# RMSNorm and QKV projection: 2x2 block products on row-tile pairs replaced by 3x2-by-2x3 block products on row-tile triples

## The chip, the cores and the metric

The kernel runs on one core of one Trainium2 chip. The metric is the device time of one execution in microseconds (us). The kernel before takes 352.87 us (median of three runs, 352.66 to 354.76).

## The reference

`x` has shape 8 x 1024 x 768 (8192 rows), `w_qkv` 768 x 2304, all in f32; `gamma` is one per column of `x`.

```
rms = np.sqrt(np.mean(x ** 2, axis=-1, keepdims=True) + eps)
x_norm = x / rms * gamma
return np.matmul(x_norm, w_qkv).astype(np.float32)
```

## The kernel before, in words

The 8192 rows are 64 row tiles of 128 rows. The contraction of 768 is six chunks (`ko`) of 128, and TensorE takes one 128x128 block of transposed x as its weights and streams a block of w past it.

The weights arrive as 16 pieces of f32 (`load_w`, L442), are multiplied by gamma and rounded to bf16 (`conv`, L448 to L452) into the tile `w_b`.

**Head.** Row tiles 0 to 3 are computed plainly: cast to bf16, transposed on TensorE (`tr`, L480), multiplied chunk by chunk with 512-wide blocks of `w_b` (`mm`, L516), scaled by 1/rms at the eviction (`evac`). Meanwhile the largest weight of each of three column groups of 768 is found (`bound`, `fold`, `bound_tr`, `bound_top`, `bound_all`), the group is divided by a scale made from it and written as four f16 quarters of 384 (k) x 384 (n) (`quad`, L616 to L618), and four differences of quarters are formed (`tsum`, L624).

**Pairs.** The other 60 row tiles go in 30 pairs. Each tile of x is loaded (`load_x`, L437), its sum of squares taken on ScalarE (`pstat`, L634), scaled to f16 on VectorE (`pcast`, L648) and transposed by a DMA (`pxbar`, L652; four of these tiles on TensorE, `ptr`, L671). A pair is a 2x2 arrangement of blocks (two row tiles, two halves of k); four sums of these blocks are formed, most on GpSimd (`osum`, L666). For each pair and each column group, seven block products (`product`, L686) replace the eight of a plain 2x2 product. A product is three matmuls of 384 columns. Products 1, 6, 7 and 4 accumulate one after the other in one PSUM bank; product 2 has a second bank, 5 and 3 a third. Between two products of a bank the running sum is read out: `hold` (L693 on VectorE, L695 on ScalarE) copies it, scaled, to an f32 tile `pp`; `join` (VectorE, L711) adds a scaled bank to a held one and writes a quarter of the result; `last` (ScalarE, L715) writes a quarter without an addition. Per pair and group that is seven readings. `pstore` (L740) stores 768 columns of a row tile; results lie in 12 tiles `ot` or in the spent `w_b`.

**The order.** `PLAN` is a list of operations with a time each; from pair 15 on, a fixed pattern over `SLOT` adds them. All are sorted by that time, and this one order is the order of every engine's queue; the engines run freely against each other and wait on semaphores. All DMAs but gamma's and one last store are issued by the SP queue. The last product is cut in two halves (`end_piece`, L722; `end_out`, L730 to L734), stored from two queues.

Of the kernel before, what the change touches and what calls it, by code (L numbers as in the profile page):

```python
# [9 lines left out]

PIECES = [(0, 2, 0, 512), (2, 3, 0, 512), (3, 4, 0, 512), (4, 5, 0, 512), (5, 6, 0, 512), (0, 2,
          512, 512), (2, 4, 512, 512), (4, 6, 512, 512), (0, 2, 1024, 512), (2, 4, 1024, 512), (4,
          6, 1024, 512), (0, 2, 1536, 512), (2, 4, 1536, 512), (4, 6, 1536, 512), (0, 3, 2048,
          256), (3, 6, 2048, 256)]

HEAD_END = 166.25
STEADY = 15

PLAN = [
    (0.000, "load_x", 1), (1.160, "load_x", 0), (1.580, "load_x", 2), (5.030, "cast", 0, "DVE"), (5.031, "load_w", 4),  # L20
    (5.032, "load_w", 1), (6.820, "cast", 2, "DVE"), (6.821, "cast", 1, "ACT"), (6.822, "stat", 0),
    (6.823, "load_w", 2), (6.824, "load_w", 3), (6.825, "gamma_in"), (6.826, "idle", 14, 512), (6.827, "tr", 1),
    (7.480, "conv", 4, 5, "DVE"), (7.481, "tr", 0), (7.482, "cp", 0, "ACT"), (7.483, "tr", 2),
    (7.484, "cp", 1, "ACT"), (8.050, "mm", 0, 0, "5"), (8.141, "conv", 1, 2, "DVE"), (8.266, "mm", 1, 0, "5"),
    (8.267, "load_x", 3), (8.801, "conv", 2, 3, "DVE"), (8.802, "cp", 2, "ACT"), (8.803, "mm", 0, 0, "2"),
    (8.926, "mm", 1, 0, "2"), (9.142, "mm", 2, 0, "5"), (9.371, "mm", 2, 0, "3"), (9.372, "stat", 1),
    (9.461, "conv", 3, 4, "DVE"), (9.587, "mm", 0, 0, "3"), (9.803, "mm", 1, 0, "3"), (10.031, "mm", 0, 0, "4"),
    (10.032, "recip", 0), (10.451, "stat", 3), (10.452, "load_w", 0), (11.772, "conv", 0, 1, "POOL"),
    (11.773, "mm", 2, 0, "4"), (11.774, "conv", 0, 0, "ACT"), (11.775, "cast", 3, "DVE"), (11.776, "mm", 1, 0, "4"),
    (11.777, "tr", 3), (12.612, "mm", 1, 0, "01"), (13.043, "mm", 0, 0, "01"), (13.044, "load_w", 6),  # L30
    (13.045, "load_w", 7), (13.046, "stat", 2), (13.047, "load_w", 5), (13.092, "conv", 6, 2, "POOL"),
    (13.093, "load_w", 10), (13.094, "cp", 3, "DVE"), (13.095, "bound", 0, 1, "DVE"), (13.831, "conv", 6, 3, "DVE"),
    (13.971, "bound", 0, 0, "ACT"), (14.261, "recip", 2), (14.262, "mm", 2, 0, "012"), (14.263, "mm", 3, 0, "012345"),
    (14.264, "load_w", 8), (14.361, "recip", 1), (15.571, "evac", 2, 0, "ACT"), (15.572, "recip", 3),
    (15.573, "load_w", 9), (17.054, "conv", 10, 5, "POOL"), (17.055, "mm", 0, 512, "23"),
    (17.056, "mm", 2, 512, "23"), (17.057, "conv", 7, 4, "DVE"), (17.058, "conv", 7, 5, "DVE"),
    (17.059, "mm", 1, 512, "45"), (17.060, "mm", 0, 512, "54"), (17.145, "mm", 3, 512, "45"),
    (17.146, "conv", 5, 1, "DVE"), (17.147, "evac", 3, 0, "ACT"), (17.576, "mm", 2, 512, "45"),
    (17.577, "load_w", 15), (17.578, "evac", 1, 0, "ACT"), (17.579, "conv", 5, 0, "DVE"),
    (18.008, "mm", 1, 512, "23"), (18.009, "bound", 1, 0, "ACT"), (18.010, "load_x", 5),  # L40
    (18.011, "bound", 0, 2, "DVE"), (18.554, "fold", 0), (18.555, "mm", 1, 512, "01"), (18.871, "bound_tr", 0),
    (18.872, "conv", 10, 4, "POOL"), (18.873, "evac", 0, 0, "DVE"), (18.971, "conv", 8, 0, "ACT"),
    (19.364, "bound_top", 0), (19.365, "load_x", 4), (19.366, "conv", 8, 1, "POOL"), (19.367, "mm", 3, 512, "01"),
    (19.695, "conv", 9, 3, "POOL"), (19.724, "bound_all", 0), (19.844, "mm", 2, 512, "01"), (20.044, "scales", 0),
    (20.045, "load_w", 14), (20.275, "mm", 1, 1024, "01"), (20.707, "mm", 3, 1024, "45"),
    (20.708, "evac", 1, 512, "ACT"), (21.139, "mm", 2, 1024, "01"), (21.140, "conv", 9, 2, "POOL"),
    (21.141, "evac", 2, 512, "ACT"), (21.142, "load_x", 7), (21.570, "mm", 0, 512, "01"),
    (22.002, "mm", 0, 1024, "23"), (22.003, "bound", 1, 2, "DVE"), (22.434, "mm", 3, 512, "23"),
    (22.435, "load_x", 6), (22.866, "mm", 2, 1024, "45"), (23.297, "mm", 3, 1024, "01"),
    (23.298, "quad", 0, "b22", "ACT"), (23.299, "quad", 0, "b12", "POOL"), (23.300, "bound", 1, 1, "DVE"),  # L50
    (23.301, "pstat", 5), (23.729, "mm", 3, 1024, "23"), (24.035, "fold", 1), (24.036, "pstat", 4),
    (24.037, "conv", 15, 3, "POOL"), (24.215, "conv", 15, 5, "ACT"), (24.216, "evac", 3, 512, "DVE"),
    (24.217, "mm", 0, 1024, "01"), (24.645, "prms", 2), (24.646, "bound_tr", 1), (24.845, "evac", 3, 1024, "DVE"),
    (24.846, "mm", 0, 1024, "45"), (24.895, "conv", 15, 4, "ACT"), (24.896, "load_w", 13), (24.897, "load_w", 12),
    (25.144, "mm", 1, 1024, "23"), (25.145, "quad", 0, "b11", "POOL"), (25.146, "load_w", 11),
    (25.325, "evac", 0, 512, "ACT"), (25.925, "evac", 0, 1024, "ACT"), (25.926, "mm", 0, 2048, "345"),
    (25.927, "mm", 1, 2048, "345"), (25.928, "bound_top", 1), (26.231, "bound_all", 1), (26.351, "mm", 1, 1024, "45"),
    (26.352, "conv", 14, 1, "POOL"), (26.353, "precip", 2), (26.354, "pcast", 5), (26.705, "conv", 14, 2, "DVE"),
    (26.965, "pcast", 4), (26.966, "pstat", 6), (26.967, "mm", 2, 1024, "23"), (26.968, "load_x", 15),
    (27.515, "tsum", 0, "t1", "DVE"), (27.516, "evac", 1, 1024, "ACT"), (27.517, "ptr", 5),  # L60
    (28.095, "conv", 13, 4, "ACT"), (28.215, "pcp", 5, "DVE"), (28.216, "conv", 14, 0, "POOL"),
    (28.217, "mm", 3, 2048, "345"), (28.218, "mm", 0, 2048, "012"), (28.735, "conv", 13, 5, "ACT"),
    (28.855, "osum", 2, "s1", "DVE"), (28.856, "mm", 3, 2048, "012"), (28.857, "mm", 2, 2048, "345"),
    (28.884, "ptr", 4), (29.244, "mm", 1, 2048, "012"), (29.572, "mm", 2, 2048, "012"),
    (29.573, "evac", 3, 2048, "DVE"), (29.574, "load_x", 12), (29.575, "pstat", 7),
    (29.818, "store", 3, 2, 2048, 256), (29.819, "scales", 1), (30.238, "load_x", 8), (30.239, "pcp", 4, "DVE"),
    (30.240, "quad", 0, "b21", "POOL"), (30.345, "evac", 0, 2048, "ACT"), (30.498, "evac", 1, 2048, "DVE"),
    (30.898, "evac", 2, 2048, "DVE"), (30.899, "mm", 1, 1536, "45"), (30.900, "conv", 12, 3, "POOL"),
    (31.038, "store", 1, 2, 2048, 256), (31.039, "conv", 12, 2, "POOL"), (31.040, "conv", 11, 0, "POOL"),
    (31.041, "quad", 1, "b21", "POOL"), (31.042, "mm", 3, 1536, "45"), (31.043, "mm", 3, 1536, "23"),  # L70
    (31.458, "store", 2, 2, 2048, 256), (31.459, "mm", 2, 1536, "23"), (31.460, "bound", 2, 1, "DVE"),
    (31.461, "conv", 11, 1, "ACT"), (31.462, "quad", 1, "b11", "ACT"), (31.626, "mm", 3, 1536, "01"),
    (32.575, "prms", 3), (32.576, "product", 2, 0, 1), (32.978, "evac", 2, 1024, "DVE"), (32.979, "product", 2, 0, 2),
    (33.033, "mm", 2, 1536, "45"), (33.034, "hold", 2, 0, "a", "p1", "ACT"), (33.638, "precip", 3),
    (33.639, "store", 0, 2, 2048, 256), (33.738, "join", 2, 0, 0, 0, "b", "p1"), (34.288, "pcast", 6),
    (34.289, "load_x", 17), (34.290, "load_x", 16), (34.291, "load_x", 11), (34.998, "osum", 2, "s2", "DVE"),
    (34.999, "mm", 0, 1536, "23"), (35.000, "mm", 1, 1536, "01"), (35.001, "mm", 2, 1536, "01"),
    (35.002, "bound", 2, 2, "ACT"), (35.003, "mm", 0, 1536, "01"), (35.191, "mm", 1, 1536, "23"),
    (35.192, "bound", 2, 0, "ACT"), (35.193, "quad", 1, "b22", "POOL"), (35.623, "product", 2, 0, 5),
    (35.624, "tsum", 0, "t2", "DVE"), (36.110, "mm", 0, 1536, "45"), (36.111, "pcast", 7),  # L80
    (36.568, "osum", 2, "s4", "DVE"), (36.569, "product", 2, 1, 1), (36.570, "pxbar", 6),
    (36.888, "osum", 2, "s3", "DVE"), (36.889, "evac", 1, 1536, "ACT"), (37.029, "product", 2, 1, 2),
    (37.030, "load_x", 23), (37.125, "hold", 2, 0, "c", "p5", "ACT"), (37.126, "quad", 1, "b12", "POOL"),
# [285 lines left out]
def kernel(  # L369
# [137 lines left out]
    def width(t, n0):  # L507
        return min(NT, N - n0)

# [328 lines left out]
```

## Time and profile before

| What | Value |
|---|---|
| median of three runs | 352.87 us |
| the profiled execution: span from first to last instruction | 352.0 us, 0.87 below the median; no other time of this execution is given |
| TensorE (PE) busy | 341.8 us, 97% |
| VectorE (DVE) busy | 265.3 us, 75% |
| ScalarE (ACT) busy | 242.1 us, 69% |
| GpSimd (POOL) busy | 118.0 us, 34% |
| granted TensorE clock | 1.000 |
| bytes moved by DMA | 119.19 MB, mean 339 GB/s |

How to read it: busy time of PE counts a matmul up to its modelled end, which overlaps the next one; the rate of the matmuls is read from their starts in the timeline. The DMA share is the busy share of the core's 16 DMA engines, summed over packets, so that it can pass 1.0 where packets overlap. SP has no compute; its rows are DMA issues.

### The profile page before, as it was taken

How to read it: one execution, taken by the hardware profiler on the slowest of the kernel's cores; microseconds unless marked ns; L12 is line 12 of the kernel's file. 1: busy time of each engine (PE TensorE's matmuls, PEld its weight loads, DVE VectorE, ACT ScalarE, POOL GpSimd, SP SyncE). 2: the span in 40 equal slices, each digit the busy share in tenths (PEclk: the TensorE clock that was granted, in tenths of full speed). 3: DMA queues.
4: the chain of work that ended last, by engine and by line, in shares of the span. 5: the costliest groups of instructions: out<-in, count | busy, mean ns of one | idle time of the engine just before them, and what ended most of it. 6: DMA issues, size and time to landing. Idle time of an engine off the chain costs nothing.

```text
span 352.0 us, 6558 instructions
## 1 busy us (share of the span) xinstructions
PE 341.8 (97%) x2079; PEld 201.4 (57%) x2082; DVE 265.3 (75%) x504; ACT 242.1 (69%) x497; POOL 118.0 (34%) x130
## 2 busy tenths in 40 slices
PE   6799999999999999999999999999999999999995
PEld 2346555666666666656666565656666666666663
DVE  2689989888788987786776859677686867767663
ACT  4999988966776756757758575766757677564543
POOL 0187237413123105244404444251614444163000
PEclk9999999999999999999999999999999999999999
DMA  7998999999999999999999999999999999998565
GB/s 267 391 383 295 311 405 309 331 313 374 314 301 374 338 411 340 371 384 314 359 374 316 404 341 365 346 386 354 356 344 326 369 327 373 314 380 301 202 260 223
DMA packets 86238, 119.19 MB, mean 339 GB/s; under 512 B 49206, under 2 KB 51132, under 8 KB 86204
## 3 DMA queue, kind: packets, MB, share of 16 engines
q1 hardware_dynamic: 86048, 118.68, 100.8%
q8 instruction: 16, 0.26, 0.3%
q14 instruction: 18, 0.15, 0.1%
q10 hardware_dynamic: 156, 0.10, 0.1%
HBM read 32.25 MB, written 75.50 MB: 306 GB/s over the span
## 4 chain that ended last, share of the span: by engine, by line
PE 92%; ACT 4%; DVE 1%; issue 1%; DMA 1%; DVEq 0%; ACTq 0%
PE pm L686 85%; PE pm L516 5%; PE pm L555 2%; ACT sq L576 1%; ACT xT L458 1%; DVE ot L711 1%; DMA g<-in_gamma_dram 1%; ACT ot L534 0%; ACT sq L467 0%; ACT pp L695 0%; PE pm L671 0%; DVE xb L648 0%; ACT w_b L450 0%; PE pm L480 0%; DVE pp L693 0%
## 5 line engine op out<-in xcount | busy, mean ns | idle before, releaser
L686 PE MATMUL pm<-wq,su 128*128 128x384 f16 x1080 | 203.8, 326 | 0.3 <-DVE pp L693 0.3
L695 ACT ACTIVATE pp<-pm,sc 128x384 f32<-128x384 f32 x207 | 116.5, 581 | 75.0 <-PE pm L686 72.7
L686 PE MATMUL pm<-wq,xT 128*128 128x384 f16 x807 | 159.3, 326 | 1.0 <-DVE ot L711 0.6
L686 PEld LDWEIGHTS <-su 128*128 128x128 f16 x1080 | 105.5, 98 | 70.1 <-issue 0.5
L711 DVE SCALAR_TENSOR_TENSOR ot<-pm,sc,pp 128x384 f32<-128x384 f32 x172 | 100.3, 611 | 23.6 <-PE pm L686 21.4
L686 PEld LDWEIGHTS <-xT 128*128 128x128 f16 x807 | 78.7, 98 | 54.1 <-issue 1.1
L666 POOL TENSOR_TENSOR su<-xT 128x384 f16<-128x384 f16 x52 | 49.6, 956 | 154.3 <-DMA xT<-xb 82.5
L711 DVE SCALAR_TENSOR_TENSOR w_b<-pm,sc,pp 128x384 f32<-128x384 f32 x98 | 58.1, 613 | 28.5 <-PE pm L686 24.5
L693 DVE TENSOR_SCALAR pp<-pm,sc 128x384 f32<-128x384 f32 x63 | 38.4, 614 | 19.1 <-PE pm L686 18.8
L634 ACT ACTIVATE sq<-x_t 128x768 bf16<-128x768 f32 x60 | 50.1, 835 | 2.1 <-DMA x_t<-in_x_dram 2.0
L648 DVE TENSOR_SCALAR xb<-x_t,rstd 128x768 f16<-128x768 f32 x60 | 41.0, 688 | 0.5
L715 ACT ACTIVATE ot<-pm,sc 128x384 f32<-128x384 f32 x48 | 27.5, 576 | 11.7 <-PE pm L686 11.7
L715 ACT ACTIVATE w_b<-pm,sc 128x384 f32<-128x384 f32 x41 | 23.4, 576 | 9.3 <-PE pm L686 9.3
L666 POOL TENSOR_TENSOR su<-su,xT 128x384 f16<-128x384 f16 x24 | 22.7, 948 | 19.6 <-DVE su L666 9.5
L516 PE MATMUL pm<-w_b,xT 128*128 128x512 bf16 (+1 forms) x117 | 25.1, 358 | 1.9 <-ACT w_b L450 0.9
L666 POOL TENSOR_TENSOR su<-xT,su 128x384 f16<-128x384 f16 x24 | 22.4, 933 | 8.7 <-DVE su L666 7.0
L516 PEld LDWEIGHTS <-xT 128*128 128x128 bf16 x120 | 11.2, 98 | 12.5 <-ACT xT L458 1.7
L452 POOL TENSOR_SCALAR w_b<-wq,g_sb 128x512 bf16<-128x512 f32 (+1 forms) x13 | 8.5, 665 | 18.0 <-DMA wq<-in_w_qkv_dram 18.0
L634 ACT ACTIVATION_READ_ACCUMULATOR sq<-x_t 128x1 f32 x60 | 11.5, 192 | 0.0
L618 POOL TENSOR_SCALAR wq<-w_b,inv 128x1152 f16<-128x1152 bf16 x8 | 10.1, 1266 | 3.2 <-issue 2.6
L638 ACT ACTIVATE rms<-ssq,eps_sb 128x2 f32<-128x2 f32 x30 | 8.8, 293 | 0.0
L573 DVE TENSOR_REDUCE bnd<-w_b 128x1 f32<-128x1536 bf16 x5 | 8.6, 1742 | 0.1
(57 smaller groups left out, 94.9 us busy)
## 6 DMA issues: line engine op xcount, KB each, us to landing
out_dram<-ot SPq DMA_DIRECT2D x110, 384.0 KB, 4.8
out_dram<-w_b SPq DMA_DIRECT2D x68, 384.0 KB, 5.0
x_t<-in_x_dram SPq DMA_DIRECT2D x64, 384.0 KB, 5.5
wq<-in_w_qkv_dram SPq DMA_DIRECT2D x10, 512.0 KB, 9.1
out_dram<-ot SPq DMA_DIRECT2D x8, 512.0 KB, 7.4
wq<-in_w_qkv_dram SPq DMA_DIRECT2D x4, 256.0 KB, 6.0
xT<-xb SPq DMA_TRANSPOSE x56, 5.0
wq<-in_w_qkv_dram SPq DMA_DIRECT2D x2, 384.0 KB, 9.5
```

The source lines that it names most:

```text
L516: nc.tensor.matmul(out=PM[t, n0][:, :nl], lhsT=XT[t][:, ko, :], rhs=w_b[:, ko, n0:n0 + nl], start=(b == 1), stop=(b == KO))
L573: nc.vector.tensor_reduce(out=o, in_=v, axis=mybir.AxisListType.XY, op=amax, apply_absolute_value=True)
L618: nc.gpsimd.tensor_scalar(out=o, in0=quad_view(c, q), scalar1=INV[c], scalar2=1.0, op0=mult, op1=mult)
L634: nc.scalar.activation(out=sq, in_=X[t], func=AF.Square, accum_out=SS[p][:, t % 2:t % 2 + 1])
L638: nc.scalar.activation(out=r, in_=SS[p], func=AF.Sqrt, scale=inv_k, bias=eps_sb)
L648: nc.vector.tensor_scalar(out=XB[t], in0=X[t], scalar1=SS[t // 2][:, t % 2:t % 2 + 1], scalar2=None, op0=mult)
L666: (nc.vector if eng == "DVE" else nc.gpsimd).tensor_tensor(out=block(p, q), in0=block(p, x), in1=block(p, y), op=op)
L686: nc.tensor.matmul(out=PB[k][:, :CW], lhsT=block(p, a)[:, ko, :], rhs=WQ[c, b][:, ko, :], start=(first and ko == 0), stop=(ko == KO // 2 - ...
L693: nc.vector.tensor_scalar(out=o, in0=pb, scalar1=SC[c], scalar2=None, op0=mult)
L695: nc.scalar.activation(out=o, in_=pb, func=AF.Copy, scale=SC[c], bias=0.0)
L711: nc.vector.scalar_tensor_tensor(out=result(p, c, i, j), in0=PB[p, c, bank][:, :CW], scalar=SC[c], in1=PART[p, c, held], op0=mult, op1=add)
L715: nc.scalar.activation(out=result(p, c, 1, 0), in_=PB[p, c, "a"][:, :CW], func=AF.Copy, scale=SC[c], bias=0.0)
```

## The change

The whole PLAN and most helpers are rewritten. The head still computes row tiles 0 to 3 plainly in bf16, now in 384-wide blocks (144 matmuls in place of 93 of 512 and 24 of 256). The other 60 row tiles go in 20 triples. A triple `g` is 384 consecutive rows; row tile `i` of it holds rows 3p+i. A triple is 3x2 blocks of x (three row tiles, two halves of k), a column half `c` (1152 columns) is 2x3 blocks of w, and 15 block products give the nine result blocks for which a plain product takes 18. The weights are scaled once per column half; 13 sums of weight blocks are formed per half (`bsum`), and 11 sums of x blocks per triple (`osum`). The 15 products run in two chains, each accumulating in one PSUM bank; after each product the bank is read once (`hold` on ScalarE six times, `join` on VectorE nine times), directly into the result tile, and a join adds in place. A triple is loaded by one DMA and transposed by one DMA; stores are 1152 columns of a row tile. Each engine's order is the order of the new PLAN, written out for all triples; PSUM banks, sum tiles and result tiles are numbered by hand. No TensorE transposes and no split last product remain after the head.

Counts, from the new PLAN: 600 products (1800 matmuls of 384 columns), 240 holds, 360 joins, 220 osums (207 on POOL, 13 on DVE), 26 bsums (18 DVE, 8 POOL), 60 pcasts (30 DVE, 30 ACT), 60 pstats. SP issues 24 loads of x, 12 of w, 20 transposes and 128 stores.

The core of the diff (the old helpers of the same names, printed above, go):

```diff
-PRODUCTS = {1: ("a11", "b11"), 2: ("a12", "b21"), 3: ("s4", "b22"), 4: ("a22", "t4"), 5: ("s1", "t1"), 6: ("s2", "t2"),
-            7: ("s3", "t3")}
+A_OF = (6, 7, 8, 9, 10, 11, 5, 12, 3, 4, 13, 14, 15, 16, 0)
+B_OF = (6, 7, 1, 5, 8, 9, 10, 11, 12, 13, 14, 15, 16, 17, 18)
+FIRST = (2, 10)
+CHAIN = (0, 0, 0, 1, 1, 1, 0, 0, 0, 1, 1, 1, 0, 1, 1)
+HW = 3 * CW
+    PS = many(8, [P, 512], f32, "ps", banks)
+    XI = many(3, [P, 3, K], f32, "xi")
+    XB = many(2, [P, 3, K], f16, "xb")
+    XT = many(3, [P, 3 * KO, P], f16, "xt")
+    SU = many(26, [P, H, P], f16, "su")
+    OUT = [spent[:, HW * j:HW * (j + 1)] for j in range(KO)] + many(8, [P, HW], f32, "ot")
+    def rows(v, g):
+        r0 = P * (N_HEAD + 3 * g)
+        return v[r0:r0 + 3 * P, :].rearrange("(p i) n -> p i n", i=3)
+    def load_t(eng, g, slot):
+        xi[g] = XI[slot]
+        nc.sync.dma_start(out=xi[g], in_=rows(xf, g))
+    def pxbar(eng, g, i0, i1, *slot):
+        nc.sync.dma_start_transpose(out=place(g, slot)[:, KO * i0:KO * i1, :], in_=xb[g][:, i0:i1].rearrange("p i k -> p (i k)"))
+    def a_block(g, i):
+        return xt[g][:, H * i:H * (i + 1), :] if i < 6 else su[g, i]
+    def osum(eng, g, f, op, i, j, slot):
+        su[g, f] = SU[slot]
+        plus(eng, su[g, f], a_block(g, i), a_block(g, j), add if op == "add" else sub)
+    def bsum(eng, c, f, op, i, j, slot):
+        wf[c, f] = WH[slot]
+        plus(eng, wf[c, f], wf[c, i], wf[c, j], add if op == "add" else sub)
+    def product(eng, g, c, r, *bank):
+        if bank:
+            po[g, c, CHAIN[r]] = PS[bank[0]][:, :CW]
+        a, b, o = a_block(g, A_OF[r]), wf[c, B_OF[r]], po[g, c, CHAIN[r]]
+        for k in range(H):
+            nc.tensor.matmul(out=o, lhsT=a[:, k, :], rhs=b[:, k, :], start=(r in FIRST and k == 0), stop=(k == H - 1),
+                             skip_group_check=True)
+    def hold(eng, g, c, r, i, sign, *slot):
+        to(eng, part(g, c, i, slot), po[g, c, CHAIN[r]], (sc if sign > 0 else nsc)[c])
+    def join(eng, g, c, r, i, sign, j, other, *slot):
+        nc.vector.scalar_tensor_tensor(out=part(g, c, i, slot), in0=po[g, c, CHAIN[r]], scalar=(sc if sign > 0 else nsc)[c],
+                                       in1=part(g, c, j), op0=mult, op1=add if other > 0 else sub)
+    def pstore(eng, g, c, i):
+        nc.sync.dma_start(out=rows(of, g)[:, i, HW * c:HW * (c + 1)], in_=ot[g, c, i])
```

Two places of the new PLAN, each item being operation, engine, triple, column half, product. The first is where the products begin:

```
bsum DVE 0 10 add 3 7 13;product PE 0 0 2 4;osum POOL 0 15 add 0 1 6;product PE 0 0 10 5;osum DVE 0 9 add 7 13 7;
hold ACT 0 0 2 2 -1 10;bsum DVE 0 13 sub 9 17 14;osum POOL 0 14 add 2 3 8;hold ACT 0 0 10 8 1 11;product PE 0 0 12;
```

The second is from the repeated part, with a piece of one triple's joins in a row:

```
pxbar SP 13 0 3 0;product PE 11 0 5;join DVE 11 0 0 1 -1 2 -1;hold ACT 11 1 12 0 1;product PE 11 1 11;
osum POOL 12 9 add 7 13 6;join DVE 11 0 5 5 -1 4 -1;product PE 11 0 1;hold ACT 11 1 11 3 1;product PE 11 1 7;
osum POOL 12 14 add 2 3 14;join DVE 11 0 1 4 1 4 1;product PE 11 0 4;join DVE 11 1 7 6 -1 8 -1;product PE 11 0 8;
osum POOL 12 15 add 0 1 4;join DVE 11 0 4 2 1 2 1;product PE 11 1 13;product PE 11 1 6;osum POOL 12 16 sub 4 14 2;
```

## The prediction

> **What bounds the kernel now.** I read the page's busy line and the chain of waits first, then the groups by line, the timeline for the step of a matmul and for the turn of a PSUM bank, and the windows for the DMA share.
>
> ```profile
> span 352.0 us, 6558 instructions
> ...
> PE 341.8 (97%) x2079; PEld 201.4 (57%) x2082; DVE 265.3 (75%) x504; ACT 242.1 (69%) x497; POOL 118.0 (34%) x130
> ...
> PE 92%; ACT 4%; DVE 1%; issue 1%; DMA 1%; DVEq 0%; ACTq 0%
> ...
> L686 PE MATMUL pm<-wq,su 128*128 128x384 f16 x1080 | 203.8, 326 | 0.3 <-DVE pp L693 0.3
> L695 ACT ACTIVATE pp<-pm,sc 128x384 f32<-128x384 f32 x207 | 116.5, 581 | 75.0 <-PE pm L686 72.7
> L686 PE MATMUL pm<-wq,xT 128*128 128x384 f16 x807 | 159.3, 326 | 1.0 <-DVE ot L711 0.6
> ```
>
> PE carries 92% of the chain, and its product matmuls waited 1.3 us in all, while ACT waited 72.7 us for them. TensorE is the bound; the readers have slack.
>
> ```profile
> 306.01 0.65 PE L686 MATMUL pm<-wq,su 128*128 128x384 f16 x3
> ...
> 309.42 0.65 PE L686 MATMUL pm<-wq,su 128*128 128x384 f16 x3
> ```
>
> Between these two starts lie seven products (21 matmuls): 3.41 us, so 0.1625 us a matmul and 0.4875 a product. The means of 326 ns include the modelled drain.
>
> ```profile
> 340.62 0.65 PE L686 MATMUL pm<-wq,xT 128*128 128x384 f16 x3
> 340.82 0.62 DVE L693 TENSOR_SCALAR pp<-pm,sc 128x384 f32<-128x384 f32 x1 [0.72 <-PE pm L686]
> ...
> 341.80 1.77 DVE L711 SCALAR_TENSOR_TENSOR ot<-pm,sc,pp 128x384 f32<-128x384 f32 x3 [0.36 <-PE pm L686]
> ...
> 346.67 1.14 DVE L711 SCALAR_TENSOR_TENSOR w_b<-pm,sc,pp 128x384 f32<-128x384 f32 x2 [0.23 <-PE pm L686]
> ...
> 347.35 0.66 PE L722 MATMUL pm<-wq,xT 128*128 128x192 f16 x6 [0.22 <-DVE w_b L711]
> ```
>
> The reader starts 0.20 us after the next product may start (340.82 against 340.62), takes about 0.60, and PE goes on 0.07 after it (346.67 + 0.61 to 347.35). So a bank turns in 0.87 us: two other products between two of one bank (0.975) hide it, one (0.4875) leaves 0.38 open, none 0.87. Readings in a row come each 0.58 us (three in 1.77).
>
> ```profile
> 10.00:30.00 20.00, 18.48 (x96) 8.64 (x99) 15.85 (x31) 18.99 (x37) 10.03 (x14) 1.00 1.05 386
> ...
> 80.00:100.00 20.00, 20.00 (x125) 12.05 (x124) 16.85 (x34) 13.88 (x31) 5.35 (x6) 1.00 1.10 345
> ...
> 180.00:300.00 120.00, 119.36 (x735) 71.61 (x733) 88.40 (x163) 81.96 (x177) 45.06 (x48) 1.00 1.07 355
> ...
> 340.00:346.00 6.00, 6.00 (x39) 3.61 (x38) 3.28 (x7) 3.63 (x7) 0.00 (x0) 1.00 0.60 241
> ```
>
> The columns are length, busy PE, weight loads, DVE, ACT, POOL, clock, DMA share and GB/s. The DMA share is 1.07 in the steady part, so DMA is the second resource that is nearly spent.
>
> **Part 1, matmuls.** Before: 1887 matmuls of 384 and six halves, 1890 x 0.1625 = 307.1; head 93 x 0.216 (starts at 35.04 and 37.63 us, 12 matmuls) + 24 x 0.109 = 22.7; 48 transposes x 0.055 = 2.6. Sum 332.4 of the 352.0 span; 19.6 us are loss. By counts of matmuls, 13.4 of it lies before 60 us (46.6 us of matmuls in it: 131 x 0.1625, and the 22.7 and 2.6), 1.3 from there to 340.13, and 4.9 after. After: 1800 x 0.1625 = 292.5; 144 head matmuls x 0.1625 = 23.4; 24 transposes 1.3. Sum 317.2. Gain 15.2 us, if the losses stay.
>
> **Part 2, the head.** SP's order puts the last of the 12 weight pieces (576 KB each) behind four x tiles (1.57 MB), the other weights (7.08 MB in all) and triple 0's x (1.18): 9.83 MB. Before, 2.82 MB had moved by 10 us and 386 GB/s after it, so its bytes are in at 28.2 us; the first 512 KB piece that POOL waited for (12.36 us) was used 1.5 us after its bytes, so 29.7. POOL converts it: 512 columns take 0.72, 256 take 0.48, so 1152 about 1.33: 31.0. The new PE order puts all head matmuls before the first product, and 52 (8.45 us) need this piece or follow one that does: first product at 39.5 us, with 24.7 us of matmuls done. Before, products filled PE from 34.06 us on beside the last head matmuls; this cover is gone. Then DVE is the queue: among the first 30 products (14.6 us of PE) it has 13 joins (7.5), 8 bsums (5.6, by 2.76 us for four), 6 osums (2.2), two quads (1.6), a 1152-wide bound (1.3) and small ones (1.1): 19.3 us, with ACT and POOL near 18 each; among the next 30 it has 14.3 against 14.6. With only two chains going in the first 11 products, seven have one or no product between them and the last of their bank (0.38 or 0.87 each), inside the same 19.3. Product 60 ends near 39.5 + 0.7 + 19.3 + 14.6 = 74.1 us with 54.0 of matmuls done: loss 20.1 in place of 13.4, +6.7. Lower end: larger packets bring the weights 1.5 us earlier and five joins may lag behind product 30 (2.9): +2.3. Upper end: three crowded queues that wait for each other cost a fifth more (19.3 becomes 23) and the second 30 products 2.4 more: +13.
>
> **Part 3, the steady part.** A triple is 30 products, 14.63 us. DVE: 18 joins x 0.58 + 2 pcasts x 0.65 + 0.2 = 11.9, 82%. ACT: 12 holds x 0.56 + 3 pstats x 1.0 + 0.3 + one pcast 0.8 = 10.8. POOL: 11 osums x 0.93 = 10.2. SP: six stores, one load, one transpose of three tiles (1.8 each): some 9. None passes PE. In the repeated order two to four products stand between two of one bank (a quarter of them two). I followed DVE through one triple: two pcasts and a precip (1.5) before the join of product 9 make it 0.5 late, and three products stand before its bank's next (slack 0.59); the next ten joins fall into 13 products, 5.8 us in 6.3, and are late by at most 0.4. So almost nothing stalls; I take +0.3 over before's 1.3, bounds 0 and 9 (rival D).
>
> The pcast and the POOL sums meet more often now.
>
> ```profile
> L648 DVE TENSOR_SCALAR xb<-x_t,rstd x60: 602/612/1344, 27.2 to 318.4; 128x768 f16<-128x768 f32 x60
> ```
>
> The median is 612 and the worst 1344 ns with POOL 34% busy; at 70% a mean of 0.8 is 0.3 us a triple. [...]
>
> The one load now lands three tiles: before, one landed in 5.0 to 6.4 us (median 5.5); 0.79 MB more at 402 GB/s adds 2.0: 7.5 us. In the new order 17 products (8.3 us) lie between load and first pstat on ACT, which would hold back the holds queued behind it. The transpose has 21 products (10.2 us), and POOL's sums are 4 us ahead of their products.
>
> **Part 4, the end.** The last ten products run in two chains with one product between: 1.36 us for two in place of 0.975, +1.5. The last store is 576 KB behind another, in place of two of 96 KB: 0.59 MB at 402 GB/s is 1.5 us against 0.25 each; with the one before it still moving, some +2.0. Before's own stall here (about 0.8) goes. Sum +2.7; bounds +2 and +4.
>
> **Sum.** 352.0 - 15.2 + 6.7 + 0.3 + 2.7 = 346.5. I add 0.6 for waits on result slots and loads between (bounds 0 and 2): 347.1. The profiled span is 0.9 below the median of its runs, so 348.0.
>
> **Rivals.**
> A, the sum above: 348, chance 0.45; its own range 345 to 351.
> B, the head costs only its lower ends: 352.9 - 15.2 + 2.3 + 2.0 + 0.5 = 342.5 to 343; for it, before reached 13.4 us of loss with DVE 97% busy from 30 to 40 us; against it, 19.3 us of DVE in 14.6. Chance 0.2.
> C, slower: the DMA queue becomes the bound. Per pair (10.24 us) share 1.07 is 10.96, of which 3.15 MB of plain traffic, at the 402 GB/s that 241 at share 0.60 gives, takes 7.83: 1.57 a transposed tile. A triple has 4.72 MB and three tiles: 11.7 + 4.7 = 16.4 in 14.63, share 1.12. If 1.07 is the ceiling, a triple takes 15.3, and 17 triples lose 12: 360. It decides as soon as the ceiling is below 1.12; against it, 80 to 100 us ran at 1.10 with PE full, and larger packets were faster (368 GB/s per share in 10 to 30 us, mostly 2 KB packets, against 402 with 3 KB), which at 4.5 KB would be about 429 and share 1.07. It shows as loads landing later than 8 us and ACT waiting for `xi`. Chance 0.2.
> D, DVE late in each triple: at 0.70 us a join the lateness of 0.5 passes its slack, and PE stalls about 0.5 a triple, 18 x 0.5 = 9: 357. For it, 82% busy in place of 74%; against it, no join row above 0.615. Chance 0.15.
>
> **Numbers.** About 1% is what a measurement of this kernel can tell from no change: 349.3 and 356.4. Of A two thirds lie below 349.3 (0.29), with B 0.49 faster; the rest of A, a fifth of C and half of D are 0.26 the same; 0.25 slower. The range 342.5 to 358 takes in B, A and most of D, and leaves out the upper part of C.
>
> **What would show it.** Right: product starts 0.1625 apart from 80 us on, PE idle there under 3 us; first product near 39.5 us, and PE idle behind DVE until 75; last PE end about 6 us before the span's end. Wrong: ACT waiting for a load or PE for POOL's sums (C), PE waiting for DVE in every triple (D), or POOL sums above 1.2 us, which would make POOL the bound.

## The result, and the profile after

The changed kernel takes 379.58 us (median of four runs, 378.12 to 380.8) against 353.38 us before: 1.0719 times the time, 95% interval 1.0672 to 1.0766. The forecast was 348.0 us, with a range of 342.5 to 358. Beside the experiments below the kernel before had medians of 353.6 to 354.4 us, so that a difference of about 1 us between two kernels says nothing. The profiled execution took 379.37 us, with a span of 377.6.

From the page of the changed kernel: busy time, the chain of work that ended last, and groups (busy us, mean ns of one, idle before and its releaser).

```profile
span 377.6 us, 5995 instructions
...
PE 334.4 (89%) x1987; PEld 194.1 (51%) x1987; DVE 297.9 (79%) x490; ACT 235.3 (62%) x455; POOL 232.8 (62%) x235
...
PE 40%; DMA 21%; DVE 7%; SPq 4%; issue 4%; ACT 2%; DVEq 0%; ACTq 0%
...
L616 PE MATMUL ps<-wh,su 128*128 128x384 f16 x1320 | 242.8, 329 | 25.4 <-DVE su L453 9.6
...
L575 ACT ACTIVATE junk<-xi 128x768 bf16<-128x768 f32 x60 | 50.4, 840 | 22.2 <-DMA xi<-in_x_dram 21.8
...
L448 DVE TENSOR_SCALAR xb<-xi,st 128x768 f16<-128x768 f32 x30 | 31.2, 1066 | 0.5
```

TensorE's share of the chain fell from 92% to 40%; DMA rose from 1% to 21%, by way of the load of `xi` that ACT's `pstat` waits for (21.8 us). The product matmuls with summed operands waited 25.4 us, before 0.3. From 100 to 340 us TensorE waited 7.4 us for ACT's holds and 3.6 for DVE's joins, while ACT waited 21.1 us for loads. The windows say where (columns: length, PE, weight loads, DVE, ACT, POOL, clock, DMA share, GB/s):

```profile
40.00:60.00 20.00, 8.90 (x38) 4.18 (x39) 19.68 (x25) 11.40 (x23) 12.71 (x11) 0.74 0.77 232
60.00:80.00 20.00, 15.39 (x82) 8.12 (x82) 19.30 (x25) 13.54 (x24) 18.45 (x10) 0.91 0.75 250
80.00:100.00 20.00, 18.40 (x113) 10.89 (x112) 17.82 (x34) 14.86 (x27) 12.34 (x12) 1.00 0.73 241
100.00:200.00 100.00, 98.19 (x601) 58.52 (x600) 77.74 (x137) 69.62 (x137) 67.50 (x75) 1.00 1.06 341
200.00:340.00 140.00, 130.50 (x789) 76.95 (x788) 109.82 (x184) 84.58 (x173) 90.69 (x98) 1.00 1.07 332
```

At 0.1625 us a matmul, 20 us hold 123 and 140 us hold 861. There are two losses of different kinds: up to 80 us DVE is full (19.68 and 19.30 of 20 us) and TensorE starved; from 200 us on the DMA share stands at 1.07 and the GB/s are lower than before.

I use one account for all kernels, that of the forecast: loss is the length of a stretch less 0.1625 us for each matmul that starts in it (0.055 for a transpose). The work is 317.2 us (322.5 and 327.8 where TensorE transposes tiles). "Product 60" is when product 61 starts.

| kernel | time, us | product 1 | product 60 | loss to 100 us | 100 to 340 | after 340 |
|---|---|---|---|---|---|---|
| forecast | 348.0 | 39.5 | 74.1 | 20.1 | 2.2 | 7.6 |
| after | 379.6 | 48.5 | 92.3 | 38.2 | 14.8 | 7.3 |
| half of the early sums to DVE | 372.8 | 40.5 | 86.1 | 32.1 | 15.4 | 7.4 |
| all early sums to DVE | 368.5 | 40.8 | 81.2 | 27.2 | 14.8 | 7.4 |
| POOL's early sums left out | 364.0 | 38.8 | 74.2 | 21.0 | 15.4 | 7.8 |
| fewer stores | 370.9 | 49.0 | 94.4 | 40.3 | 6.5 | 7.7 |
| no transpose DMAs | 371.1 | 50.2 | 93.4 | 39.4 | 5.2 | 7.5 |
| one tile of three on TensorE | 374.8 | 48.4 | 92.2 | 38.2 | 5.1 | 7.5 |
| all sums to DVE, one tile on TensorE | 364.9 | 41.7 | 82.8 | 28.8 | 4.6 | 7.4 |
| all sums to DVE, no transpose DMAs | 359.5 | 40.6 | 81.6 | 27.5 | 5.4 | 7.4 |
| neither POOL's sums nor transposes | 352.9 | 38.6 | 75.8 | 22.1 | 5.3 | 7.5 |

The forecast's row is its own sum: 13.4 + 6.7, 1.3 + 0.3 + 0.6, and 4.9 + 2.7. In all kernels with the head as changed, the loss to 100 us came out at 37.7 to 40.5, so differences of up to 3 us in that column say nothing.

My theory from these views has two parts. S: in the head, DVE and POOL hold each other up while both add 16-bit tiles in SBUF. D: in the steady part the DMA engines are the bound, because a triple asks for more of them than TensorE's new, shorter time gives (not to be confused with the prediction's rival D, which is DVE late in each triple; an expectation that sets another theory against it calls it "rival D"). The timeline of the changed kernel's head speaks for S (start, duration, engine; in brackets the idle time before and its releaser):

```profile
39.00 1.42 POOL L453 TENSOR_TENSOR su<-xt 128x384 f16<-128x384 f16 x1
39.58 1.46 DVE L453 TENSOR_TENSOR wh<-wh,wh 128x1152 f16<-128x1152 f16 x1
...
44.51 1.46 DVE L453 TENSOR_TENSOR wh<-wh,wh 128x1152 f16<-128x1152 f16 x1
45.32 2.86 POOL L453 TENSOR_TENSOR wh<-wh,wh 128x1152 f16<-128x1152 f16 x1
...
45.89 2.50 DVE L453 TENSOR_TENSOR su<-xt,su 128x384 f16<-128x384 f16 x1
...
48.45 1.46 PE L616 MATMUL ps<-wh,su 128*128 128x384 f16 x4 [9.59 <-DVE su L453]
```

A 128x384 sum, counted at 0.36 us, takes 2.50 us while POOL works at one long sum, and a 128x1152 sum 1.46 in place of 0.69. The head matmuls were done at 38.86 us, near the forecast's place; TensorE then waited 9.59 us for DVE.

The ends of these rows say more than their lengths. POOL's first sum ends at 40.42 us (39.00 + 1.42) and DVE's wide one 0.62 us later; POOL's long sum ends at 48.18 and DVE's small one 0.21 us later. So it is in the whole trace of this kernel: all 13 wide DVE sums that began during a sum of POOL ended 0.61 or 0.62 us after that sum, all five 128x384 ones 0.21 or 0.22 after it, and the five wide ones that met none took 0.74 on average. In these rows the two engines take turns, as far as ends can show it: no DVE sum that met one of POOL ended before it. Of the joins, 211 began during a sum of POOL, and none took more than 0.62 us.

### The profile page after: what moved, and what is told of

Its sections match the earlier page's. It is cut to its first block, busy times and chain, and to the rows that moved or that the text cites. A ratio compares the mean times of both kernels' runs of the same rounds, so it can differ in the third digit from the quotient of the medians.

```text
span 377.6 us, 5995 instructions
## 1 busy us (share of the span) xinstructions
PE 334.4 (89%) x1987; PEld 194.1 (51%) x1987; DVE 297.9 (79%) x490; ACT 235.3 (62%) x455; POOL 232.8 (62%) x235
## 4 chain that ended last, share of the span: by engine, by line
PE 40%; DMA 21%; DVE 7%; SPq 4%; issue 4%; ACT 2%; DVEq 0%; ACTq 0%
PE ps L616 40%; DMA xi<-in_x_dram 21%; SPq L632 4%; DVE ot L628 4%; DVE xb L448 2%; ACT junk L575 1%; DVE w_b L628 1%; DVE wh L453 1%; ACT ot L443 1%; ACT w_b L443 0%; DVE st L581 0%; ACT st L578 0%; DVEq L628 0%; ACTq L443 0%
## 5 line engine op out<-in xcount | busy, mean ns | idle before, releaser
L616 PE MATMUL ps<-wh,su 128*128 128x384 f16 x1320 | 242.8, 329 | 25.4 <-DVE su L453 9.6
L628 DVE SCALAR_TENSOR_TENSOR ot<-ps,sc,ot 128x384 f32<-128x384 f32 x216 | 126.9, 613 | 40.3 <-PE ps L616 36.2
L453 POOL TENSOR_TENSOR su<-xt 128x384 f16<-128x384 f16 x113 | 106.6, 957 | 83.8 <-DMA xt<-xb 44.5
L443 ACT ACTIVATE ot<-ps,sc 128x384 f32<-128x384 f32 x144 | 79.9, 578 | 60.2 <-PE ps L616 58.6
L616 PE MATMUL ps<-wh,xt 128*128 128x384 f16 x480 | 99.8, 326 | 5.0 <-DVE ot L628 4.6
L628 DVE SCALAR_TENSOR_TENSOR w_b<-ps,sc,w_b 128x384 f32<-128x384 f32 x144 | 84.7, 613 | 23.0 <-PE ps L616 22.1
L443 ACT ACTIVATE w_b<-ps,sc 128x384 f32<-128x384 f32 x96 | 53.8, 578 | 39.1 <-PE ps L616 38.2
L616 PEld LDWEIGHTS <-xt 128*128 128x128 f16 x480 | 46.9, 98 | 38.4 <-issue 8.3
L575 ACT ACTIVATE junk<-xi 128x768 bf16<-128x768 f32 x60 | 50.4, 840 | 22.2 <-DMA xi<-in_x_dram 21.8
L453 POOL TENSOR_TENSOR su<-xt,su 128x384 f16<-128x384 f16 x57 | 55.5, 973 | 5.3 <-DVE su L453 2.9
(49 smaller groups left out, 81.2 us busy)
## 6 DMA issues: line engine op xcount, KB each, us to landing
ot<-in_w_qkv_dram SPq DMA_DIRECT2D x12, 576.0 KB, 11.1
```

The costliest lines, as they stand in the source:

```text
L443: nc.scalar.activation(out=out, in_=in_, func=AF.Copy, scale=scale, bias=0.0)
L453: (nc.vector if eng == "DVE" else nc.gpsimd).tensor_tensor(out=out, in0=in0, in1=in1, op=op)
L575: nc.scalar.activation(out=junk[:, :K], in_=xi[g][:, i], func=AF.Square, accum_out=ST[g % 6][:, i:i + 1])
L616: nc.tensor.matmul(out=o, lhsT=a[:, k, :], rhs=b[:, k, :], start=(r in FIRST and k == 0), stop=(k == H - 1), skip_group_check=True)
L628: nc.vector.scalar_tensor_tensor(out=part(g, c, i, slot), in0=po[g, c, CHAIN[r]], scalar=(sc if sign > 0 else nsc)[c], in1=part(g, c, j), ...
```

## The experiments

### Half of the early sums to DVE

```diff
-bsum POOL 0 15 add 0 1 4;
+bsum DVE 0 15 add 0 1 4;
...
-osum POOL 0 6 add 1 5 0;
+osum DVE 0 6 add 1 5 0;
...
```

So for all of POOL's block sums of column half 0 (three, by the PLAN) and all of its sums of triple 0 (seven); the counts in the expectation are too high.

> The sums of weight blocks of the first column half and of x blocks of triple 0 go from POOL to DVE (5 bsums' and 9 osums' worth of queue), nothing else. Theory S (DVE and POOL slow each other in the head: in the changed kernel a DVE bsum took 1.42 us in place of 0.75, a quad 1.37 in place of 0.81, with POOL busy 10.0 of 10 us between 30 and 50 us): although DVE gets more to do, its bsums fall back to about 0.75 and osums to 0.35, the first product comes near 42 us in place of 48.45, and the run gains 4 to 8 us. Rival V (the volume of sums is the bound, not the overlap): DVE gets some 6 us more, the first product comes no earlier than 50 us, the run loses 2 to 6 us.

372.83 us (372.64 to 373.92), 1.0536 [1.0494, 1.0578] of before: 6.8 us faster than the changed kernel, although DVE has more to do. DVE's wide sums took 0.844 us on average from 38 to 60 us. From 60 to 78 us, where POOL still adds column half 1, this group of the same kernel shows

```profile
L453 DVE TENSOR_TENSOR wh<-wh,wh 128x1152 f16<-128x1152 f16 x7 | 12.9, 1858 | 0.0
```

so the slow sums moved to where POOL adds. S stands, and the next experiment follows from it.

### All early sums to DVE

The same for column half 1 and triple 1.

> All block sums of the weights (both column halves) and the triple sums of triples 0 and 1 run on DVE; POOL keeps its conversions and quads in the head and all sums from triple 2 on. Theory S (DVE and POOL slow each other while both add): the column half 1 sums, which took 2.7 us each on POOL and stretched DVE's to 1.7 to 2.4 us between 60 and 78 us, fall to about 0.75 us each on DVE; products done between 60 and 80 us rise from 75 matmul groups to about 95, and the time falls by another 4 to 6 us, to 367 to 369 us. Rival Q (the queue, not the contention): 11 more sums of about 0.6 us are 6 to 7 us more in DVE's queue between 55 and 85 us, and the time stays at 371.5 us or above.

368.45 us (367.68 to 371.66), 1.0431 [1.0375, 1.0486]. Groups from 38 to 80 us, first of the changed kernel, then of this one:

```profile
L453 DVE TENSOR_TENSOR wh<-wh,wh 128x1152 f16<-128x1152 f16 x16 | 22.3, 1413 | 0.0
...
L453 POOL TENSOR_TENSOR wh<-wh,wh 128x1152 f16<-128x1152 f16 x5 | 13.7, 2769 | 0.0
...
L628 DVE SCALAR_TENSOR_TENSOR ot<-ps,sc,ot 128x384 f32<-128x384 f32 x17 | 10.0, 611 | 1.0 <-PE ps L616 0.5
```

```profile
L628 DVE SCALAR_TENSOR_TENSOR ot<-ps,sc,ot 128x384 f32<-128x384 f32 x31 | 18.0, 611 | 1.1 <-issue 0.3 <-PE ps L616 0.3
L453 DVE TENSOR_TENSOR wh<-wh,wh 128x1152 f16<-128x1152 f16 x21 | 15.2, 754 | 0.0
```

21 wide sums now take less time than 16 did: 754 ns against 1413. The joins, which read one operand from PSUM, take 611 ns in both: they are not slowed. Product 60 comes 11 us sooner. Seven us are left to the forecast's 74.1, and DVE is still full (19.58 of 20 us from 60 to 80), now with POOL's sums in its own queue.

### POOL's early sums left out

All of POOL's block sums (eight, by the PLAN) and its sums of triples 0 and 1 are left out and nobody else makes them; the products read an existing block. This separates the length of DVE's queue from the changed order of the head.

```diff
 def bsum(eng, c, f, op, i, j, slot):
+    if eng == "POOL":
+        wf[c, f] = wf[c, 1]
+        return
 def osum(eng, g, f, op, i, j, slot):
+    if eng == "POOL" and g < 2:
+        su[g, f] = a_block(g, 1)
+        return
```

> POOL's sums before triple 2 (seven block sums of the weights and its sums of triples 0 and 1) are left out, and the products that need them use one of the existing blocks, so those rows are not the reference's; DVE keeps exactly its own order of the changed kernel and takes none of POOL's. Theory S2 (the forecast's queue of DVE was counted rightly but for POOL's presence; the 8 us that stay when DVE takes the sums over are the price of the longer DVE queue): DVE's own sums take 0.75 and 0.36 us, the first product starts at about 40 us, product 60 ends near 74 us as forecast, and the time is 360 to 364 us. Rival L (the lost cover and the two-chain start cost more than the forecast had, whoever adds): the time stays at 367 to 370 us, as with all the sums on DVE.

363.95 us (361.08 to 365.6), 1.0285 [1.0227, 1.0343]. The timeline at the first product, and the window from 60 to 80 us:

```profile
37.74 0.75 DVE L453 TENSOR_TENSOR wh<-wh,wh 128x1152 f16<-128x1152 f16 x1
...
38.40 0.35 DVE L453 TENSOR_TENSOR su<-xt,su 128x384 f16<-128x384 f16 x1
...
38.67 0.75 DVE L453 TENSOR_TENSOR wh<-wh,wh 128x1152 f16<-128x1152 f16 x1
...
38.81 0.66 PE L622 MATMUL ps<-wh,su 128*128 128x384 f16 x3 [0.55 <-DVE su L453]
```

```profile
60.00:80.00 20.00, 19.82 (x123) 11.84 (x121) 18.33 (x36) 16.94 (x33) 8.12 (x9) 1.00 1.11 303
```

With DVE's own work unchanged and POOL not adding beside it, product 60 is at 74.2 us, forecast 74.1; product 30 at 59.2, forecast 59.5 (39.5 + 0.7 + 19.3); TensorE is full from 60 to 80 us. The lost cover and the start in two chains were, taken together, priced right. The 18 us by which product 60 was late are all POOL's sums: 11 us come back when DVE makes them itself, the other 7 are what making them takes. The run leaves out waits for POOL's results too, but the changed kernel had none of weight: from 38 to 100 us its TensorE waited 17.2 us for DVE, 1.1 for ACT and none for POOL, and DVE waited for TensorE alone (2.4 us). Nor were the DMAs what slowed DVE: without POOL's sums the DMA share was higher, 1.05 from 38 to 50 us and 1.01 from 50 to 60, in place of 0.98 and 0.55.

### Matmuls of zeros in the gap

The granted clock fell to 0.63 between 40 and 50 us of the changed kernel. 40 matmuls of zeros ahead of the first product keep TensorE busy while it waits.

```diff
-product PE 0 0 2 4;
+idle PE 40 512 0;product PE 0 0 2 4;
```

> 40 matmuls of zeros (512 columns, into a bank that no product uses) are put on PE before the first product, where it stood idle for 9.6 us. Theory C (the granted clock fell to 0.63 to 0.91 between 40 and 80 us because PE stood idle, and the products there ran slower for it): the clock stays at 1.00, matmul steps there are 0.163 us, and the run gains 2 to 5 us. Rival: the stretch is bound by DVE and POOL, so that the clock costs nothing: clock 1.00, gain under 1 us.

381.16 us (379.61 to 382.5), no gain. Product 1 started at 48.3 us as before. The clock was 0.90 from 40 to 60 us in place of 0.74, but 0.84 from 60 to 80 us in place of 0.91, so the condition of theory C, a clock of 1.00, was not reached, and this run alone does not exclude C. Two other numbers speak against it: DVE was busy 19.68 and 19.30 us of these two stretches in the changed kernel, and in the kernel without transpose DMAs (below) the clock was 1.00 from 60 to 80 us, while products 1 to 60 still took 43.2 us, in the changed kernel 43.8.

### Loads issued earlier

From triple 3 on each load is issued right behind the transpose of the triple two before it.

```diff
 pxbar SP g-2 0 3 slot;
+load_t SP g slot;
...
-load_t SP g slot;
```

> Only SP's order changes: from triple 4 on, the load of a triple is issued right behind the transpose that stood one transpose earlier, ahead of the stores between, some 5 us or more sooner. Theory L (in the part from 100 to 340 us, 14 us are lost because the load's lead is too short: ACT waits 21 us for it in 14 places, 9.3 us median from issue to landing): ACT's waits for the loads fall under 3 us, the loss in that part falls under 4 us, the run gains 8 to 12 us. Rival D (the DMA queue is full, share 1.07): what the loads gain, transposes and stores lose; waits move to POOL's sums or to result slots, gain under 3 us.

383.48 us (381.54 to 384.5), 1.0832 [1.0782, 1.0883]: 3.9 us slower. SP's queue shows why. Start and duration, the changed kernel first, the early loads second:

```profile
236.82 8.92 SPq L594 DMA_TRANSPOSE xt<-xb  x1
245.79 1.05 SPq L632 DMA_DIRECT2D out_dram<-ot  x2
246.93 2.25 SPq L632 DMA_DIRECT2D out_dram<-w_b  x2
249.23 1.22 SPq L632 DMA_DIRECT2D out_dram<-ot  x1
250.49 1.27 SPq L572 DMA_DIRECT2D xi<-in_x_dram  x1
251.86 1.13 SPq L632 DMA_DIRECT2D out_dram<-w_b  x1
253.17 7.96 SPq L594 DMA_TRANSPOSE xt<-xb  x1
```

```profile
236.89 10.95 SPq L596 DMA_TRANSPOSE xt<-xb  x1
247.89 0.57 SPq L574 DMA_DIRECT2D xi<-in_x_dram  x1
...
252.87 10.47 SPq L596 DMA_TRANSPOSE xt<-xb  x1
```

SP issues with no pause in both, and these rounds take 16.35 and 15.98 us (by the count of matmuls from 100 to 340 us the mean is 15.58 and 15.81) where TensorE needs 14.63. The loads landed in 7.0 us in place of 9.3 and ACT waited for none, but the transposes landed in 11.0 in place of 9.4, and ACT waited 12.3 us for stores to free result slots. The wait moved; the queue was not shorter. That is D's sign, and this change of order does not help.

### One transpose split into three

```diff
-pxbar SP g 0 3 slot;
+pxbar SP g 0 1 slot;pxbar SP g 1 2;pxbar SP g 2 3;
```

> Each triple's one transpose DMA becomes three of one row tile, issued one behind the other at the same place. Theory N (the one large DMA is no cause by itself; a tile costs 2.3 us of SP's time either way): SP is held as long, the time is within 1.5 us of the changed kernel. Rival T (one DMA of three tiles holds SP and the DMA queue for 7 to 9 us, and this makes loads and sums late): first tiles land earlier, waits of POOL and ACT for DMA fall, the run gains 3 to 8 us.

381.0 us (379.76 to 382.05): no gain. From 236 to 262 us the three together held SP 9.18 and 8.65 us, one 8.92 and 7.96. The single large DMA, a named part of the change, is not the cause.

### Fewer stores

Column half 1 of triples 3 to 17 is not stored.

```diff
-pstore SP g 1 i;
```

> The stores of column half 1 of triples 3 to 17 are left out (1.77 of 4.72 MB of plain traffic a triple), so that part of the output is not written; nothing else changes. Theory D (the DMA engines are the bound of the steady part): plain traffic falls from 11.7 to about 7.3 us of the 14.63 us triple, the loads land in under 7 us, ACT's waits for loads fall from 21 us to under 3 us, the loss between 100 and 340 us falls from 14 us to under 4 us, and the time is 366 to 370 us. Rival W (the waits come from the transposes or the order, whatever the traffic): the loads' waits stay above 12 us and the time above 375 us.

370.86 us (369.41 to 373.56), 1.0491 [1.0431, 1.0551]. ACT's waits for loads fell from 21.1 to 3.6 us, the loss from 100 to 340 us from 14.8 to 6.5. The direction and the size are D's, though the loss stayed above the 4 us, the loads' landing (7.9 us) above the 7, and the time just above the 370, that I had written.

### No transpose DMAs

```diff
 def pxbar(eng, g, i0, i1, *slot):
+    if g > 4:
+        return place(g, slot)
```

> The transpose DMAs are left out from triple 5 on (the products then use what the buffers held before, so the output from there on is not the reference's); loads, stores, casts, sums and products all stay. Theory T (a transposed tile holds the DMA engines for about 1.6 us, 4.7 us a triple, far more than its 11% of the bytes): the DMA share between 100 and 340 us falls to 0.75 to 0.85, loads land in under 6 us, the loss there falls from 14 us to under 4 us, and the time is 366 to 370 us. Rival B (bytes alone count): the share falls by a tenth only, to about 0.95, and the time, since that just fits, is 368 to 374 us.

371.07 us (369.35 to 371.43), 1.0478 [1.0438, 1.0518]. The page's line of SP's DMA queue (packets, MB, share of 16 engines over the span), of the changed kernel and of this one, and this one's window:

```profile
q1 hardware_dynamic: 70336, 119.55, 97.3%
```

```profile
q1 hardware_dynamic: 35296, 110.70, 84.5%
```

```profile
200.00:340.00 140.00, 137.37 (x837) 81.45 (x836) 114.89 (x194) 88.68 (x177) 90.61 (x95) 1.00 0.85 309
```

45 transposed tiles less take 0.973 x 377.6 - 0.845 x 369.3 = 55 us of the 16 engines' time away, 1.23 us a tile, though only 7% of the bytes. The packets of 256 bytes, which only the transposes of the changed kernel have, add up to 75.5 us of the 16 engines' time for its 60 tiles, 1.26 a tile. So a tile costs more than its bytes (B), but less than T's 1.6: the share over 100 to 340 us is 0.88, between T's 0.85 and B's 0.95, and the time lies in B's range and above T's. From 200 us on the share is 0.85 and TensorE is nearly full; between 100 and 340 us it still waited 3.0 us for DVE's joins, and 5.2 us are lost, not the under 4 expected. The loads landed in 8.8 us, not under 6, and ACT still waited for them no more than 2.5 us in all.

Put as a rate, a tile's 196.6 KB in 1.23 us of all 16 engines are 160 GB/s, beside 309 / 0.85 = 364 for the plain traffic of this run.

### Loads and stores on two queues

```diff
-load_t SP g slot;
+load_t ACT g slot;
...
-pstore SP g 0 i;
...
+pstore ACT g 0 i;
```

> From triple 3 on the loads, and up to triple 17 the stores of column half 0 (ten steps later in the order), are issued on ACT's queue, so that plain packets of a second queue can run while SP's queue works at a transpose. Theory H (the hole of some 1.3 us beside each transpose in which SP's queue moves nothing is what is lost): the period of a triple falls from 16.35 us towards 14.63, and the time is 370 to 376 us. Rival E (the engines are shared, a transpose holds them whatever the queue): the time is within 2 us of 379.6. Rival K (ACT, blocked in issuing, delays its holds): slower, 384 us or more.

381.32 us (379.19 to 384.3), 1.0773 [1.0693, 1.0852]: within 2 us of the changed kernel, rival E. The DMA share was 1.06 to 1.07 again: here a second queue found no engine time that the first had left.

### One tile of three transposed on TensorE

```diff
-pxbar SP g 0 3 slot;
+pxbar SP g 0 2 slot;
...
+ptr PE g 2 0;
...
+pcp ACT g 2;
```

From triple 4 on; the transposes on TensorE stand 20 steps of the order behind the DMA, the copy 7 behind them.

> From triple 4 on the third tile of each triple is transposed on PE (six transposes into the free PSUM bank, copied out by ACT) and the DMA transposes two tiles. Theory D: a transposed tile takes about 1.35 us of DMA share, so a triple's DMA need falls from about 16 to 14.7 us, while PE's grows by 6 x 0.055 = 0.33 us, 5.3 us over 16 triples; ACT's waits for loads fall from 21 us to under 6 us and the time from 379.6 to 373 to 377 us. Rival: if the stalls are not made by the DMA's amount of work, the 5.3 us come on top: 383 us or more.

374.84 us (374.17 to 375.1), 1.0578 [1.0555, 1.06]: 4.7 us faster than the changed kernel, though TensorE has 5.3 us more to do. ACT's wait for loads and the window:

```profile
ACT junk L580 <- DMA xi<-in_x_dram: 0.9, 1, 0.9
```

```profile
200.00:340.00 140.00, 136.92 (x872) 82.75 (x871) 112.35 (x191) 93.09 (x184) 89.86 (x98) 1.00 0.98 327
```

21.1 us of waiting are 0.9, and the share is 0.98. Only who transposes the third tile (and, with it, when it lands) is changed, so this is the plainest evidence for D. Fewer stores, no transposes and fewer transposes have in common that they take work from the DMA engines, and each brings the loss from 100 to 340 us to 5.1 to 6.5 us; another order, another size and another queue leave the amount of work, and the loss there is 18.0, 16.1 and 18.5.

### Both causes at once

Three kernels have all early sums on DVE, and from there on: one tile of three on TensorE; two tiles on TensorE; no transpose DMAs.

> All block sums of the weights and the triple sums of triples 0 and 1 on DVE, and from triple 4 on one tile of three transposed on PE. If the two causes are separate (one lies before 100 us, the other behind), the gains add: 368.5 minus 3 to 6, 362 to 366 us, still slower than the kernel before. If the earlier start of the steady part only meets the DMA limit sooner, the gain of the transposes on PE is larger, 358 to 362 us.

364.9 us (363.87 to 365.88), 1.03 [1.0271, 1.0329]: the gains of 11.1 and 4.7 us nearly add. It is the fastest of those that leave nothing out, and still slower than before.

> As the kernel with the sums on DVE and one tile of three transposed on PE, but two tiles of three on PE. If one tile is enough to bring the DMA under its ceiling, the second only costs PE 6 x 0.055 x 16 = 5.3 us: 4 to 6 us slower than with one tile. If the DMA is still the bound with one tile, the second gives back about as much as it costs: within 2 us.

369.83 us (369.05 to 370.54): 4.9 us slower than with one tile, 5.3 expected for the added transposes. One tile was enough to bring DMA under its ceiling here: with it the share was 1.03 from 100 to 200 us and 0.97 from 200 to 340.

> All block sums of the weights and the triple sums of triples 0 and 1 on DVE, and no transpose DMAs from triple 5 on (the products use what the buffers held, so the output from there on is not the reference's). It takes both suspected causes away at once. If they are separate and the only ones of size, the gains of 11 us and 8.5 us add: 359 to 361 us; what is left above the forecast of 346.5 us of span is then about 12 us, and its place shows in the windows. If the DMA limit had also hidden a part of the head's gain: 355 to 358 us.

359.54 us (357.73 to 359.85), 1.0135 [1.0098, 1.0172]: 368.45 - 8.5 was expected to be 360. The causes are separate.

### Neither POOL's early sums nor transposes

This leaves out POOL's early sums, as above, and the transpose DMAs from triple 5 on.

> The same, and the transpose DMAs are left out from triple 5 on too (the products then use what the buffers held). If the forecast's sum was right but for POOL beside DVE in the head and the DMA limit in the steady part, this is the kernel that it described: 347 to 354 us. If a third cause is left, 357 us or more.

352.88 us (352.19 to 354.01, ten runs), 0.9974 [0.9955, 0.9992]. Its loss is 35.0 us, the forecast's 29.9, and none of what is left is large: 2.0 in the head, 3.1 between. Even with both costs gone, and with sums that the result needs left out, the kernel is only as fast as before.

## Why the forecast was wrong, step by step

**What bounds the kernel before** was right but read too narrowly. TensorE carried the chain, but the DMA share of 1.07 was not merely "nearly spent": no kernel here with the steady part as changed kept more than that from 100 to 340 us (1.05 to 1.07), and in the four of them that the table has, TensorE lost 14.8 to 15.4 us there. Before, a tile took 10.24 / 2 = 5.12 us. After, 1386 product matmuls started from 100 to 340 us, 15.4 triples, so 15.58 us a triple and 5.19 a tile. TensorE needs 4.88. The steady part gained nothing.

**Part 1** (15.2 us less matmul work) was right: the counts are as forecast, and with both costs taken away the loss comes to within 5.1 us of the forecast's.

**Part 2, the head, +6.7 (bounds +2.3 to +13), measured +24.8** (38.2 - 13.4). The step that failed is the 19.3 us of DVE's queue: its durations, four sums in 2.76 us and 0.36 for a small one, came from a place of the kernel before where POOL was idle (from 35.66 to 41.95 us), while the same sentence has POOL at 18 us beside it.

```profile
38.43 2.76 DVE L624 TENSOR_TENSOR wq<-wq 128x1152 f16<-128x1152 f16 x4
```

Beside POOL's sums the wide sum took 1.41 us in place of the 0.69, because DVE's sums waited POOL's out: those that met one ended 0.61 or 0.62 us after it. The forecast had reckoned with POOL beside DVE for the pcast alone (a mean of 0.8 us beside a median of 612 ns). The count of instructions, the order and the first product were right, as the run without POOL's sums shows (38.8 and 74.2 us). The upper bound allowed a fifth more for "crowded queues"; the factor for the wide sums is 1.9 (1413 against 754 ns).

By what DVE read, the rows differ: sums of two SBUF tiles took 1.9 times as long beside POOL's (1413 against 754 ns), joins with one input in PSUM no longer (611 ns in both). The conversions `wh<-w_b`, with one input and from SBUF, were longer too: from 30 to 60 us they took 1555 ns on average in the changed kernel and 701 without POOL's sums.

**Part 3, the steady part, +0.3 and +0.6, measured +13.5** (14.8 - 1.3). The join counts and the engine loads held: with DMA relieved some 5 us are lost, inside the bounds of 0 to 9, and 3.0 of them are waits for DVE's joins. What failed is the choice between A and C. A, and with it the +0.3 and +0.6, let a share of 1.12 through; what the runs showed in its place is a triple of 15.58 us, held by the DMA engines. C's need of 16.4 us was right in sum, 15.58 us at a share of 1.065 are 16.6, but partly by luck: its plain traffic was too cheap (11.7, at 364 GB/s 13.0) and its transposes too dear (4.7, at 1.23 a tile 3.7). C's ceiling of 1.07 was right too. Of its signs ACT's wait for `xi` was the telling one; loads landing later than 8 us (9.3) told little, since they took 8.2 and 8.8 us where DMA had been relieved. I set C at 0.2 because 20 us had run at 1.10 with TensorE full. A short stretch does not decide this: the changed kernel itself lost only 2.7 us from 100 to 200 us, at a share of 1.06, and 12.1 from 200 to 340, at 1.07. That tiles landed earlier carried the first stretch is my reading; no run tests it, nor why 20 us can run at 1.10. The hope that packets of 4.5 KB bring 429 GB/s at a share of 1 was wrong: it was 364. The pcast's mean, forecast at 0.8, was 1.07 us; DVE at 78% absorbed it.

**Part 4, the end, +2.7, measured +2.4** (7.3 - 4.9). The last matmul ended 5.3 us before the span's end, forecast about 6.

**The rivals.** C was right for the steady part with 360, and the head's 18 us lay on top. B did not come. D's mechanism exists but costs some 3 us. No rival had the head's real cost, so the two errors added to 30.5 us of span: 18.1 + 12.6 - 0.3, rounded.

## What to carry to other kernels

Before crediting a faster engine, write down what each unit of work asks of the second resource, and divide by the share at which that resource ran while the first was full: if the profile already stands at that share over the long stretch, the saved time may have nowhere to go. Here the share stood at 1.07 from 180 to 300 us, and a tile took 5.12 us before and 5.19 after. Take a duration only from a place where the neighbours do what they will do in the new place; two queues that are each counted at their lone speed are no bound when their instructions wait for each other, as the wide sums did (1413 ns beside POOL's, 754 without). Moving a transposed tile from DMA to the matrix engine won here, 4.7 us, though that engine was nearly full (130.50 of 140 us busy from 200 us on): 0.33 us of TensorE bought 1.2 us of DMA. With DMA under its ceiling it no longer won: the second tile cost 4.9 us.

## What the runs showed of the hardware that I had not expected

- A 128x1152 16-bit sum on DVE took 0.75 us alone and 1.41 us on average beside POOL's sums (1.86 in the worst stretch); POOL's own took 2.77. In the changed kernel DVE's ended 0.61 to 0.62 us after the sum of POOL that ran when they began, all 13 of them. So adding on both engines was slower than adding on DVE alone: 368.45 against 379.58 us for the whole kernel.
- A transposed 128x768 tile took 1.23 us of the DMA engines here (one DMA for three tiles or three DMAs gave the same time within 0.4%), and three kept SP for 8 to 9 us in the full queue shown above.
- TensorE's granted clock fell to 0.63 from 40 to 50 us, most of which was the wait of 9.6 us; filling the wait with 40 matmuls brought no time back (381.16 against 379.58 us).
